# Dilated attention: order of the combination, of the transposes and of the last half-tiles

## The chip, the cores and the metric

The kernel runs on one core of a Trainium2 chip. The metric is the device time of one execution in microseconds (us), the median of several runs. The core has five engines with queues of their own: TensorE (PE in the profile, its weight loads PEld), VectorE (DVE), ScalarE (ACT), GpSimd (POOL) and SyncE (SP), which here issues the DMA transfers. Each engine works through its instructions in the order in which they stand in its queue, and semaphores hold an instruction back until what it needs is there.

## The reference

One encoder block on a sequence of 1024 tokens with 1024 channels. Three mixers work side by side on the normalised input: a dilated window attention, a grouped-query attention with rotary positions, and a cross-attention into 256 memory tokens. Each mixer's output is multiplied by a gate, projected by a branch matrix (`w_br_a`, `w_br_b`, `w_br_m`), merged with sigmoid gates and projected by `w_out`; a norm and the residual follow. All data are float32.

The change concerns the dilated attention. It has three groups of eight heads, with window and dilation (128, 1), (512, 4) and (2048, 16); each gives an output and a log-denominator per token and head, and the three are combined by a softmax over the log-denominators:

```python
for gi, (window, dil) in enumerate(A_GROUPS):
    hs = slice(gi * A_HEADS, (gi + 1) * A_HEADS)
    o_g, lse_g = dilated_window_attention(aq[:, :, hs], ak[:, :, hs], av[:, :, hs], window, dil)
    outs.append(o_g)
    lses.append(lse_g)
wts = jax.nn.softmax(jnp.stack(lses, axis=0), axis=0).astype(dt)
oa = jnp.einsum('gbsh,gbshd->bshd', wts, jnp.stack(outs, axis=0)).reshape(b, s, BRANCH_WIDTH)
...
ya = (oa * jax.nn.silu(ga)) @ w_br_a[layer]
```

## The kernel before

A float32 product runs on TensorE as three products of a high and a low part (high x high, high x low, low x high). The parts come from "splits": ScalarE copies the high part (L1342 for a weight tile, L1863 `dl_high` for a mixer's output), and another engine subtracts it to get the low part (L1343 on VectorE or GpSimd, L1866 `dl_low` on GpSimd).

From L887 on the order of the instructions on every engine is the order in which the program writes them. The stage in question (L1992, `weave(16, every(), ...)`, about 1062 to 1264 us after the span's start) interleaves two streams by counters of cost. One stream is sixteen branch projections (`add_y(m)`, m = 0 to 15, matmuls at L1885, 24 each). Around them run the load of a weight tile, its split (on GpSimd for m + 1, so the split of m = 14 is due during m = 13), the load of a gate and the evacuation on VectorE (L1360 to L1365); these are kept in a list `pend`, of which one is taken after every second matmul.

The other stream is the attention, in twelve items n = 0 to 11: pairs of heads p_ = 0 to 3, for each the groups g = 0 to 2. An item has eight blocks of 128 queries, T = 0 to 7. It runs as a software pipeline over the previous item `pre` and the current one `it`, in four visits b = 0 to 3, each followed by two "rest" pieces T = 2b and 2b + 1. A visit puts on TensorE the scores of two blocks (L1561 to L1573), and transposes of probabilities of an earlier pair of blocks (L1608): of the previous item in visits 0 and 1, of the current one in visits 2 and 3. VectorE masks the scores (L1585) and copies the transposes (L1614); ScalarE takes the exponential (L1586). In visit 1 the previous item's statistics are transposed and copied by ScalarE (`stats`, L1663 to L1670, into the tile sr). In visit 2 the previous item's values are multiplied (`pv`, matmuls L1627 or L1637 to L1647, evacuated by ScalarE at L1657), and the values of the current item are loaded (tile avs). Banks of PSUM come from rings; `pst()` hands out the next of four.

After the third group of a pair of heads is through, its combination begins with visit 2 of the item that follows. Its steps are a list in `combine`, and `STEP_T` gives for each step the piece T at which it is written: fetch the statistics (SyncE), `shares` (VectorE L1798 to L1801, ScalarE), `weights` (VectorE), `put` (SyncE L1814), the loads of two weight tiles wgt (SyncE L1786), `weigh(0)` and `weigh(1)` (products on GpSimd, L1822), `weigh(1, True)` (a sum on GpSimd, L1820), `load(2)`, `load_gate` (L1830), `weigh(2)`, its sum, `gate` (GpSimd L1825) and `store` (SyncE L1833). The tile wgt has two buffers, so a later load waits until an earlier product is done. A step that is written at a T smaller than its predecessor's is that of the next item. The stored parts come back as hl and are split by `dl_high` and `dl_low`.

The last pair of heads (p_ = 3) is combined without memory. TensorE spreads the weights over PSUM banks (`wide(g, x)`, for group g and half x of the columns), `first_two(x)` adds the first two groups, and `third(x)` adds the third on VectorE (L1971, L1972), multiplies by the gate on GpSimd (L1973) and splits the half (L1863, L1866). The list in `ending()` sets their order. Behind the stage, projections m = 16, 17 and 18 start at L2027 with half of their products each, in three pairs of PSUM banks, two of which hold spreads of the last pair of heads.

Of the kernel before, what the change touches and what calls it, by code (L numbers as in the profile page):

```python
# [9 lines left out]
R = mybir.dt.float32r  # L10
# [5 lines left out]
S = 1024  # L16
NT = 8
P = 128
# [15 lines left out]
def block(ctx: ExitStack, tc: tile.TileContext, x, xT, memT, cst, msk, bcst, tabA, gpost,  # L34
          wu, wv, wb, wmem, wbr, wout, out):
    nc = tc.nc
    V, A, G, PE = nc.vector, nc.scalar, nc.gpsimd, nc.tensor
# [10 lines left out]
    bank = {}  # L48
# [14 lines left out]
    def pss1():  # L63
        return bank["p"].tile([P, 512], F32, name="s1", tag="s1", bufs=bank["n"][1])

    def pst():
        bank["i"] += 1
        return bank["p"].tile([P, 4, 128], F32, name="tr", tag="t", bufs=bank["n"][2])
# [149 lines left out]
    def pool(name, side="left"):  # L218
        p = tc.tile_pool(name=name, bufs=1, side=side, reuse_waits="tile")
        return p, p.__enter__()  # L220
# [673 lines left out]
    qkp, qk = pool("qk")  # L894
# [25 lines left out]
    def parts_of(t):  # L920
        return t if type(t) is tuple else (t[:, lo], t[:, hi])
# [289 lines left out]
    for n in range(28):  # L1211
        i, k = divmod(n, 4)
# [47 lines left out]
    for n in range(28):  # L1260
        i, k = divmod(n, 4)
# [77 lines left out]
    def y_split(m, E=V, t=None):  # L1339
        if m < len(steps):  # L1340
            t = t or wp.tile([P, 1024], R, name="wh")
            A.activation(t[:, lo], YW[m][:, lo], AF.Copy)  # L1342
            E.tensor_tensor(t[:, hi], YW[m][:, lo], t[:, lo].bitcast(F32), op=OP.subtract)  # L1343
            YW[m] = [z.rearrange("p (k f) -> p k f", k=4) for z in parts_of(t)]
# [126 lines left out]
    with ExitStack():  # L1471
# [10 lines left out]
        def pickers():  # L1482
            i96 = ident[0:96, 0:96]
            V.tensor_reduce(pick, i96.rearrange("p (x t) -> p t x", t=NT), axis=AX.X, op=OP.add)
            V.tensor_reduce(each, i96.rearrange("p (x t) -> p x t", t=NT), axis=AX.X, op=OP.add)
            V.tensor_tensor(each[:, 0:6], each[:, 0:6], each[:, 6:12], op=OP.add)
            V.tensor_copy(spread.rearrange("p g h q -> p (g h) q"), each[:, 0:6, None].to_broadcast([96, 6, 64]))

        def qk_fetch(p_, g):

            d = OPS[p_, g] = {}
            for j, x in enumerate("qk"):
                d[x] = qk.tile([P, S], F32, name="a" + x, bufs=2)
                nc.sync.dma_start(d[x], qkd[j, p_, g])
# [197 lines left out]
        def plan(it, pre, nxt):  # L1692

            out = []

            def combining(T):
                while todo and T == todo[0][0]:
                    todo.pop(0)[1]()

            def tokens(T):  # L1700
                n = seq.index(it["key"])
                if (n, T) == (1, 7):
                    pickers()
                if 1 <= n <= 4 and 4 <= T <= 6:
                    (lambda: b_high(n - 1, lo), lambda: b_high(n - 1, hi), lambda: b_low(n - 1))[T - 4]()
                if (n, T) in ((0, 2), (0, 6), (1, 3), (2, 3)):
                    b_load(((0, 2), (0, 6), (1, 3), (2, 3)).index((n, T)))
                if n in (8, 9) and T == 5:
                    dl_load(n - 8)
                if n in (9, 10) and T < 3:  # L1710
                    dl_high(n - 9, half[T]) if T < 2 else dl_low(n - 9)
                if n == 11:
                    if T == 6:
                        DL["g"] = cb.tile([P, S], F32, name="wgt", bufs=2)
                        nc.sync.dma_start(DL["g"], g2d[0, 3])
                    if T in (2, 3):
                        j = T - 2
                        nc.sync.dma_start(rows[32 * j:32 * j + 32], std[3, j].rearrange("s h (t a) -> (s h t) a", t=NT))

            def ready():  # L1720
                if pre and pre["key"][1] == 2:
                    todo.extend(zip(STEP_T, combine(pre["key"][0], [OG.pop((pre["key"][0], x)) for x in range(3)])))

            def visit(b):
                at = it if b > 1 else pre

                def turning():
                    return at["trans"]((b + 2) % 4) if at and (it or b < 2) else []

                copies = turning() if b == 1 or not it else []  # L1730
                if it:
                    it["scores"](b)
                if b == 2 and pre:
                    pre["pv"]()
                for f in copies:
                    f()
                copies = turning() if b != 1 and it else []
                if b == 1 and pre and it:
                    pre["stats"]()
                if it:  # L1740
                    it["soft"](2 * b)
                    it["soft"](2 * b + 1)
                for f in copies:
                    f()
                if not it:
                    return
                if b == 2:
                    it["values"]()
                if b == 2 and pre:
                    ready()  # L1750
                if b == 3 and it["ahead"]:
                    qk_fetch(*it["ahead"])

            def rest(T):
                if T == 3 and pre:
                    pre["send"]()
                combining(T)
                if T == 5 and it["key"][1] < 2:
                    it["turned"]()
                tokens(T)  # L1760

            for b in range(4):
                out.append((lambda b=b: visit(b), SOFT + 100.0 if it else 0.5 * LAST_PAD))
                if not it:
                    out.append((lambda b=b: shares_3(b), 0.5 * LAST_PAD))
                else:
                    out += [(lambda T=T: rest(T), 0.5 * SOFT + 50.0) for T in (2 * b, 2 * b + 1)]
            return out
# [67 lines left out]
                    lambda: weigh(1, True), lambda: load(2), load_gate, lambda: weigh(2), lambda: weigh(2, True), gate] + [store] * (p_ < 2)  # L1836

        todo = []
        STEP_T = (5, 0, 2, 3, 3, 7, 0, 1, 1, 4, 5, 6, 7, 1)
        seq = [(p_, g) for p_ in range(4) for g in range(3)]  # L1840
        items = [item(*x) for x in seq] + [None]

# [4 lines left out]
        def b_load(k):  # L1847
            nc.sync.dma_start(OPER[1][1][k].bitcast(F32), od[1, k])

        def b_high(k, t):  # L1850
            h, l = [x[k][:, t] for x in OPER[1]]
            A.activation(h, l.bitcast(F32), AF.Copy)

        def b_low(k):
            h, l = [x[k] for x in OPER[1]]
            G.tensor_tensor(l, l.bitcast(F32), h.bitcast(F32), op=OP.subtract)

        def dl_load(k):
            nc.sync.dma_start(hl[k].bitcast(F32), od[0, k])
            DL[k] = hl[k].bitcast(F32)  # L1860

        def dl_high(k, t=slice(0, S)):
            A.activation(hh[k][:, t], DL[k][:, t], AF.Copy)  # L1863

        def dl_low(k, t=slice(0, S)):
            G.tensor_tensor(hl[k][:, t], DL[k][:, t], hh[k][:, t].bitcast(F32), op=OP.subtract)  # L1866
# [86 lines left out]
                dl_low(2)  # L1953

        def wide(g, x):
            while (g == 2 or x) and bank["i"] % 4 != (2 + x if g == 2 else g):
                pst()
            W3B[g, x] = pst().rearrange("p a b -> p (a b)") if g == 2 or x else pss1()
            PE.matmul(W3B[g, x], spread[:, g].rearrange("p h q -> p (h q)"), C["w"][0:96, half[x]], start=True, stop=True)

        def first_two(x):
            t = half[x]
            a, b = C["ogs"]
            V.tensor_tensor(W3B[0, x], W3B[0, x], a[:, t], op=OP.mult)
            V.tensor_tensor(a[:, t], W3B[1, x], b[:, t], op=OP.mult)
            V.tensor_tensor(a[:, t], W3B[0, x], a[:, t], op=OP.add)

        def third(x):
            t = half[x]
            a, b = C["ogs"][0], OG[3, 2]  # L1970
            V.tensor_tensor(W3B[2, x], W3B[2, x], b[:, t], op=OP.mult)  # L1971
            V.tensor_tensor(a[:, t], W3B[2, x], a[:, t], op=OP.add)  # L1972
            G.tensor_tensor(a[:, t], a[:, t], DL["g"][:, t], op=OP.mult)  # L1973
            dl_high(3, t)
            dl_low(3, t)

        def ending():
            DL[3] = C["ogs"][0]
            return [(lambda: [wide(g, 0) for g in range(2)], 500.0), (lambda: [wide(g, 1) for g in range(2)], 500.0),
                    (lambda: [first_two(0), wide(2, 0)], 2500.0), (lambda: [first_two(1), wide(2, 1)], 2500.0),  # L1980
                    (lambda: [third(0), y_split(18, V, qk.tile([P, S], R, name="aq", bufs=2))], 2500.0),
                    (lambda: third(1), 2500.0)]

        def every():
            yield from first()
# [358 lines left out]
```

## Time and profile before

| | |
|---|---|
| median of three runs | 1389.47 us (1388.53 to 1391.44) |
| profiled execution | 1393.69 us |
| its span | 1391.9 us |
| mean granted TensorE clock | 0.993 |
| TensorE busy | 1361.3 us, 98% of the span |
| VectorE busy | 1013.2 us, 73% |
| ScalarE busy | 653.8 us, 47% |
| GpSimd busy | 579.7 us, 42% |

The profile is of one execution. Times count from the start of its span; 1.8 us of the execution lie around the span. An instruction is named by the line of the kernel that wrote it, by its engine, and by its tiles as "out<-in". A bracket at the end of a row says how long the engine was idle before it and what ended that. A row of waits reads: who waited, for whom, us in total, how often, the longest. A row of windows gives a stretch of time with the busy time of each engine in it and the TensorE clock that was granted, 1.00 being full speed.

### The profile page before, as it was taken

What the parts mean: (1) busy time and instruction counts of PE and PEld (TensorE: products, weight loads), DVE (VectorE), ACT (ScalarE), POOL (GpSimd) and SP (SyncE); (2) the same over time, 40 slices, a digit from 0 to 9 for tenths busy, and PEclk for the clock granted to TensorE, in tenths of its full rate; (3) what the DMA queues carried; (4) which work ended last, traced back from release to release, by engine and by line L of the source; (5) the groups of instructions that cost most, each with busy time, mean ns of one, the idle gap of its engine ahead of it and who ended that gap; (6) DMA issues with size and microseconds to landing.
All of it is one profiled execution on the core that took longest, in us unless ns stands there. A gap on an engine that the chain in (4) does not pass through costs nothing.

```text
span 1391.9 us, 22846 instructions
## 1 busy us (share of the span) xinstructions
PE 1361.3 (98%) x8303; PEld 1091.7 (78%) x8303; DVE 1013.2 (73%) x1840; ACT 653.8 (47%) x1384; POOL 579.7 (42%) x443
## 2 busy tenths in 40 slices
PE   7999999999999999999999999999999999998997
PEld 7799987666666789988888888888887777777886
DVE  7768767777777498766787776688777667667977
ACT  6454456656655345323333334333335776652332
POOL 0507702676576100254556554456551244561003
PEclk9999999999999999999999999999999999999999
DMA  6355532222244678524233333333338777876455
GB/s 233 97 192 188 187 123 102 99 79 93 72 130 140 218 232 262 173 68 135 78 114 117 111 108 119 121 114 100 96 122 268 241 201 226 264 198 207 148 190 182
DMA packets 125489, 213.81 MB, mean 154 GB/s; under 512 B 32480, under 2 KB 64576, under 8 KB 125376
## 3 DMA queue, kind: packets, MB, share of 16 engines
q1 hardware_dynamic: 116064, 198.42, 44.4%
q10 hardware_dynamic: 9312, 13.93, 2.8%
q8 instruction: 65, 1.06, 0.3%
q14 instruction: 48, 0.39, 0.1%
HBM read 145.92 MB, written 66.38 MB: 153 GB/s over the span
## 4 chain that ended last, share of the span: by engine, by line
PE 84%; DMA 4%; DVE 3%; POOL 3%; ACT 2%; issue 2%; SPq 1%; DVEq 0%; POOLq 0%; ACTq 0%
PE s L1309 35%; PE d L1885 4%; PE s L1219 4%; PE s L2109 4%; PE ov L804 3%; PE sc L2027 3%; PE s L1270 3%; PE d L128 3%; PE d L132 3%; PE d L130 3%; PE tr L770 2%; PE s L789 2%; PE s L788 2%; DMA avs<-vdr 2%; PE d L2109 2%
## 5 line engine op out<-in xcount | busy, mean ns | idle before, releaser
L795 POOL TENSOR_TENSOR bl<-bl,bp 128x512 f32<-128x512 f32 x96 | 133.1, 1386 | 54.2 <-ACT bp L791 48.7
L1309 PE MATMUL s<-hh,vS 128*128 128x512 f32 x400 | 133.4, 395 | 0.0
L1309 PE MATMUL s<-vA,vS 128*128 128x512 f32 x450 | 106.6, 390 | 0.0
L91 DVE TENSOR_TENSOR vS<-vot,vS 128x512 fp32r<-128x512 f32 x75 | 86.2, 1150 | 19.9 <-ACT vS L90 19.9
L1309 PEld LDWEIGHTS s<-vA,vS 128*128 128x128 f32 x450 | 84.5, 188 | 18.3
L791 ACT ACTIVATE bp<-s 128x512 f32<-128x512 f32 x128 | 75.7, 596 | 43.6 <-PE s L789 42.5
L771 DVE TENSOR_REDUCE bn<-tr 128x1 f32<-128x512 f32 x128 | 84.9, 683 | 13.4 <-PE tr L770 12.0
L1585 DVE CUSTOM_DVE_ANT_0 pra<-s,mask 128x192 f32<-128x192 f32 (+1 forms) x192 | 49.7, 309 | 59.9 <-PE s L1573 26.3
L128 PE MATMUL d<-hh,wh 128*128 128x512 f32 x224 | 90.0, 402 | 2.4 <-DVE fth L201 2.4
L132 PE MATMUL d<-hh,wl 128*128 128x512 f32 x224 | 90.1, 402 | 0.0
L130 PE MATMUL d<-hl,wh 128*128 128x512 f32 x224 | 89.3, 399 | 0.0
L1309 PEld LDWEIGHTS s<-hh,vS 128*128 128x128 f32 x400 | 75.3, 188 | 17.7
L1586 ACT ACTIVATE pra<-pra,sts 128x192 f32<-128x192 f32 (+1 forms) x176 | 72.4, 414 | 16.0 <-DVE sts L1585 15.8
L1309 PE MATMUL s<-hl,vS 128*128 128x512 f32 x200 | 79.1, 395 | 0.0
L1309 PE MATMUL s<-hh,wh 128*128 128x512 f32 x200 | 78.4, 392 | 0.0
L1309 PE MATMUL s<-hh,wl 128*128 128x512 f32 x200 | 78.4, 392 | 0.0
L1309 PE MATMUL s<-hl,wh 128*128 128x512 f32 x200 | 77.8, 389 | 0.0
L1313 ACT ACTIVATE vv<-s 128x512 f32<-128x512 f32 x50 | 30.0, 599 | 85.6 <-PE s L1309 59.1
L1053 POOL TENSOR_TENSOR vot<-wr 128x512 f32<-128x512 f32 x13 | 22.2, 1705 | 111.8 <-DVE wl L91 111.8
L804 PE MATMUL ov<-bp,VS 128*64 128x512 f32 x256 | 58.5, 598 | 0.0
L1053 POOL TENSOR_TENSOR vot<-vot,vA 128x512 f32<-128x512 f32 x12 | 19.3, 1609 | 90.7 <-DVE vS L91 90.7
L128 PEld LDWEIGHTS d<-hh,wh 128*128 128x128 f32 x224 | 42.6, 190 | 16.3 <-issue 5.5
(627 smaller groups left out, 4016.2 us busy)
## 6 DMA issues: line engine op xcount, KB each, us to landing
wr<-in_wu SPq DMA_DIRECT2D x40, 512.0 KB
vA<-in_wu SPq DMA_DIRECT2D x24, 512.0 KB
qkd<-ko SPq DMA_DIRECT2D x96, 128.0 KB
wl<-thd SPq DMA_DIRECT2D x24, 512.0 KB
wos<-os SPq DMA_DIRECT2D x12, 512.0 KB
wr<-in_wbr SPq DMA_DIRECT2D x24, 256.0 KB
aq<-qkd SPq DMA_DIRECT2D x12, 512.0 KB
ak<-qkd SPq DMA_DIRECT2D x12, 512.0 KB
```

What stands on the lines that cost most here:

```text
L91: V.tensor_tensor(dst_l, src, dst_h.bitcast(F32), op=OP.subtract)
L128: PE.matmul(dst, wh[:, k, :], hh[k][:, t], start=k == 0, stop=False)
L130: PE.matmul(dst, wh[:, k, :], hl[k][:, t], start=False, stop=False)
L132: PE.matmul(dst, wl[:, k, :], hh[k][:, t], start=False, stop=k == 7)
L771: fp["last"] = V.tensor_reduce(st[i]["n"][:, j, c:c + 1], s, axis=AX.X, op=OP.min)
L791: A.activation(pp, s, AF.Exp, scale=-1.0)
L795: G.tensor_tensor(lsum[i % 2], lsum[i % 2], pp, op=OP.add)
L804: PE.matmul(o[e * 64:e * 64 + 64], VS[:, kt, kv], d.pop(kt), start=kt < 2, stop=kt >= NT - 2)
L1219: PE.matmul(now[j], a, b, start=k == 0 and q == 0, stop=k == 3 and q == 2)
L1309: PE.matmul(BANK[n, c], a, b, start=k == 0 and q == 0 and not more, stop=k == 3 and q == 2, skip_group_check=c in "XW")
L1586: A.activation(src, src, AF.Exp, scale=-1.0, bias=bias, accum_out=sts[:, 1, h, T:T + 1])
L2109: PE.matmul(dst[:, e[0]:e[1]], a, b, start=k == 0 and q == 0, stop=k == 3 and q == 2)
```

## The change

Four things are moved; no arithmetic is added or removed.

1. In visit 2 the transposes of the current item's first two blocks are written before the previous item's values; before, they were written after them.
2. `STEP_T` has other pieces. Listed by step: `shares` T 0 to 1, `weigh(0)` 7 to 6, `weigh(1)` 0 of the next item to 7, its sum 1 to 0, `load(2)` 1 to 0, `load_gate` 4 to 3, `weigh(2)` 5 to 3, its sum 6 to 4, `gate` 7 to 6. Fetch, weights, put, the first loads and the store stay where they were.
3. The spreads of the last combination are put at other places of the ring of banks.
4. The two halves of the third term follow each other, and the split of weight tile m = 18 comes after the second half; before, it stood between the halves.

```diff
@@ visit
                 if it:
                     it["scores"](b)
-                if b == 2 and pre:
-                    pre["pv"]()
                 for f in copies:
                     f()
                 copies = turning() if b != 1 and it else []
+                if b == 2 and pre:
+                    pre["pv"]()
@@ combine
-        STEP_T = (5, 0, 2, 3, 3, 7, 0, 1, 1, 4, 5, 6, 7, 1)
+        STEP_T = (5, 1, 2, 3, 3, 6, 7, 0, 0, 3, 3, 4, 6, 1)
@@ wide
-            while (g == 2 or x) and bank["i"] % 4 != (2 + x if g == 2 else g):
+            while (g == 2 or x) and bank["i"] % 4 != {(0, 1): 3, (1, 1): 1, (2, 0): 2, (2, 1): 0}[g, x]:
                 pst()
@@ ending
-                    (lambda: [third(0), y_split(18, V, qk.tile([P, S], R, name="aq", bufs=2))], 2500.0),
-                    (lambda: third(1), 2500.0)]
+                    (lambda: third(0), 2500.0),
+                    (lambda: [third(1), y_split(18, V, qk.tile([P, S], R, name="aq", bufs=2))], 2500.0)]
```

## The prediction

> **What bounds the kernel now.** I read the page's busy times first, then TensorE's grouped waits over the stage that the change touches (us 860 to 1290 hold nothing else that stops TensorE for long), then the windows around these waits, then the timelines of single engines there.
>
> ```profile
> PE 1361.3 (98%) x8303; PEld 1091.7 (78%) x8303; DVE 1013.2 (73%) x1840; ACT 653.8 (47%) x1384; POOL 579.7 (42%) x443
> ```
> ```profile
> PE sc L2027 <- DVE og L1972: 3.6, 1, 3.6
> PE tr L1637 <- DMA avs<-vdr: 2.6, 3, 2.0
> PE s L1565 <- DVE sts L1585: 1.8, 2, 1.1
> PE tr L1608 <- ACT sr L1670: 1.5, 1, 1.5
> PE d L1885 <- POOL wh L1343: 0.3, 1, 0.3
> ```
>
> TensorE is busy 98% of the span, so only what changes a wait of TensorE, or its clock, changes the time. The second view (total us, times, longest us) lists all there is to win directly: 3.6 + 2.6 + 1.8 + 1.5 + 0.3 = 9.8 us. The clock adds to that. In the windows the columns are PE, PEld, DVE, ACT, POOL busy, granted clock, DMA share, GB/s:
>
> ```profile
> 1199.00:1202.41 3.41, 1.88 (x20) 1.50 (x17) 1.17 (x6) 3.02 (x12) 3.41 (x3) 1.00 1.04 413
> 1202.41:1205.82 3.41, 3.41 (x35) 2.42 (x34) 2.26 (x8) 3.41 (x11) 1.83 (x1) 0.50 0.83 281
> 1212.65:1216.06 3.41, 2.34 (x23) 1.78 (x21) 3.22 (x16) 1.85 (x6) 0.62 (x1) 1.00 0.94 324
> 1216.06:1219.47 3.41, 3.41 (x100) 3.10 (x100) 0.63 (x5) 1.54 (x7) 1.74 (x1) 1.00 0.90 309
> 1229.72:1233.13 3.41, 1.27 (x20) 1.03 (x22) 0.38 (x4) 0.00 (x0) 3.33 (x2) 1.00 1.09 310
> 1233.13:1236.54 3.41, 3.41 (x55) 2.85 (x52) 0.22 (x3) 0.49 (x1) 1.44 (x1) 0.50 0.44 92
> 1263.85:1267.26 3.41, 3.19 (x8) 2.55 (x9) 2.13 (x4) 1.95 (x4) 2.52 (x2) 0.50 0.72 228
> ```
>
> After a window with 1.53 us idle (3.41 − 1.88) or 2.14 us idle (3.41 − 1.27), and after the 3.6 us wait, the next 3.41 us are granted 0.50; after one with 1.07 us idle (3.41 − 2.34) they are granted 1.00. So a stall costs its own length, and from somewhere between 1.07 and 1.53 us inside one window also a slow stretch behind it.
>
> What a slow stretch costs, and the other TensorE rows (start, duration, waits in brackets):
>
> ```profile
> 1197.91 1.11 PE L1627 MATMUL tr<-app,avs 64*64 64x64 f32 x64
> 1200.75 0.52 PE L1608 MATMUL tr<-cs,pra 64*128 64x64 f32 x10 [1.53 <-ACT sr L1670]
> 1232.30 2.51 PE L1637 MATMUL tr<-app,avs 128*64 128x128 f32 x28 [1.97 <-DMA avs<-vdr]
> 1235.81 0.48 PE L1608 MATMUL tr<-cs,pra 64*128 64x64 f32 x4
> 1238.33 0.34 PE L1608 MATMUL tr<-cs,pra 64*128 64x64 f32 x4
> 1244.00 0.40 PE L1885 MATMUL d<-bh,wh 128*128 128x512 f32 x1
> 1257.54 0.39 PE L2027 MATMUL sc<-hh,wh 128*128 128x512 f32 x1
> 1260.07 0.39 PE L2027 MATMUL sc<-hh,wh 128*128 128x512 f32 x1
> 1264.07 0.76 PE L2027 MATMUL sc<-hh,ak 128*128 128x512 f32 x1 [3.61 <-DVE og L1972]
> 1268.39 0.39 PE L2027 MATMUL sc<-hh,aq 128*128 128x512 f32 x1
> ```
>
> The same four transposes take 0.48 us at clock 0.50 and 0.34 us at 1.00, so 0.29 of their slow time is lost. Over a stretch that is at least 3.41 × 0.29 = 1.0 and at most 3.41 × 0.50 = 1.7 us. I take 1.3.
>
> **The change, part by part.** Four edits, each costed on the profiled execution (1393.69 us, span 1391.9), which is 4.2 us above the median of the three runs (1389.47); the sum is then taken off the median. No instruction is added or removed on any engine, nor any DMA (allocations that only turn the ring of banks aside), so every term is a wait that moves.
>
> *Gate one piece earlier.* The 0.3 us wait for GpSimd's L1343 (the split of m = 8, which stands behind the gate there) goes: −0.3.
>
> *Transposes ahead of values, third visit.* The ten transposes at 1200.75 take 0.52 us and wait for the statistics' copy, which ScalarE does late, behind dl_high. Today the values' 64 matmuls (1.11 us) are issued before that wait and use the time; afterwards they stand behind it and the transposes. What is in cover becomes exposed: 1.11 − 0.52 = +0.6. The 1.53 us itself and its slow stretch stay. Where the values wait for a load (1232.30), it is the other way: the four transposes (0.34) fill the wait, −0.35. The same happens in front of 1184.60 (0.45 us in a timeline row), but what follows there waits again, so I take 0. The VectorE waits of L1565 (1.8) keep their work ahead: 0, bounded by −1.8 and, if all of the transposes' copies come late instead, +0.6.
>
> *Combination's steps.* SyncE's queue holds the rest: the store of a finished part waits there for the gate, and everything behind it on SyncE (weights out, loads of weights, values) with it.
>
> ```profile
> SPq L1833 <- POOL og L1825: 9.5, 2, 5.0
> ```
>
> The store waits 9.5 us in two places. The gate one piece earlier takes about 1.0 us off that chain, and with it off the landing of the values that TensorE waits for at 1232.30. Bounds: −2.16 (all of 1.97 and of the 0.19 just ahead of it) and +0.6, if the gate's load, which now goes ahead of the values' loads on SyncE, delays them by its own issue. I take −1.0, as the queue ahead is the nearest row. With the 0.35 that leaves 0.8 us idle, under the 1.07 that did no harm, so the slow stretch of 1233.13 goes too: −1.3. Running sum: −0.3 + 0.6 − 0.35 − 1.0 − 1.3 = −2.35.
>
> Then a wait is added. On GpSimd the split of m = 14 stands today between the third product and the last sum; afterwards the sum is ahead of it:
>
> ```profile
> 1237.86 2.96 POOL L1822 TENSOR_TENSOR og<-og,wgt 128x1024 f32<-128x1024 f32 x1 [3.29 <-DMA wgt<-wgd]
> 1240.75 1.30 POOL L1343 TENSOR_TENSOR wh<-wr,wh 128x512 fp32r<-128x512 f32 x1
> 1242.00 2.40 POOL L1820 TENSOR_TENSOR og<-og 128x1024 f32<-128x1024 f32 x1
> ```
>
> The product starts at its load's landing, 1237.86 − 1.0 for the earlier chain = 1236.9; + 2.96 + 2.40 + 1.30 = 1243.5. TensorE needs the split at its third matmul of m = 14, today at 1244.00, then at 1244.0 − 2.35 = 1241.65. That is a new stall of 1.9 us, and the gain up to there shrinks to −0.45. Bounds: no stall if the load lands 1.9 us earlier (−2.35), a stall of 2.9 if it lands no earlier (+0.55). With 1.7 us of the idle time in the window 1239.95 to 1243.36 (the grid of the windows above) a slow stretch follows: +1.3.
>
> *The third term's halves in a row, and the banks.* Today the split of m = 18 (ScalarE copy, VectorE L1343) stands between the halves on VectorE; it waits 2.59 us for ScalarE's copy, that one stands behind dl_high, which waits for GpSimd. The second half, and the bank that m = 17 wants, come only after it.
>
> ```profile
> 1256.62 0.69 DVE L1972 TENSOR_TENSOR og<-tr,og 128x512 f32<-128x512 f32 x1
> 1259.90 1.36 DVE L1343 TENSOR_TENSOR aq<-wr,aq 128x512 fp32r<-128x512 f32 x1 [2.59 <-ACT aq L1342]
> 1261.18 0.68 DVE L1363 SCALAR_TENSOR_TENSOR d<-wl,d 128x512 f32<-128x512 f32 x1
> 1261.90 0.69 DVE L1365 TENSOR_TENSOR acc<-d,acc 128x512 f32<-128x512 f32 x1
> 1263.23 0.69 DVE L1972 TENSOR_TENSOR og<-tr,og 128x512 f32<-128x512 f32 x1
> ```
> ```profile
> 1258.72 0.63 ACT L1863 ACTIVATE hh<-og 128x512 fp32r<-128x512 f32 x1 [5.50 <-POOL og L1973]
> 1259.26 0.61 ACT L1342 ACTIVATE aq<-wr 128x512 fp32r<-128x512 f32 x1
> ```
> ```profile
> 1257.39 1.29 POOL L1973 TENSOR_TENSOR og<-og,wgt 128x512 f32<-128x512 f32 x1 [3.44 <-DVE og L1972]
> 1259.43 1.28 POOL L1866 TENSOR_TENSOR hl<-og,hh 128x512 fp32r<-128x512 f32 x1 [0.74 <-ACT hh L1863]
> ```
>
> Afterwards VectorE ends half 0 at 1257.31, does the two evacuations (1.4), and ends half 1 at 1257.31 + 1.4 + 1.4 = 1260.1. m = 17 would start on TensorE at 1260.3 (m = 16's last matmul, 1260.07, + 0.23), so its 3.61 us wait goes whichever bank it has; the new bank numbers I cost at 0 for that reason, and if half 1 were not done they would cost up to the 3.6. Late next is m = 18's split. GpSimd: half 0 to 1258.7, its dl_low to 1260.7, half 1's product to 1262.05. ScalarE: dl_high to 1262.7, the copy to 1263.2. VectorE's L1343 then runs beside GpSimd's dl_low, as the row above did (1.36), to 1264.65. m = 18 starts at 1264.75. TensorE would be there at 1260.3 + 2.76 = 1263.06 (2.76 is m = 16's 1257.54 to 1260.30), so 1.7 us of stall. Today m = 18 starts at 1268.39: −3.64. Bounds: −4.3 with L1343 at 0.68, and −2.1 if a slow stretch follows the new stall (today's m = 17 took 4.32 instead of 2.76, so 1.5 lost). The stall lies across the edge at 1263.85, 0.8 in one window and 0.9 in the other: I take none.
>
> **Sum**: −0.45 + 1.3 − 3.64 = −2.8. Against the profiled execution 1390.9; against the median 1389.47 − 2.8 = 1386.7.
>
> **The rivals.**
> 1. *Neither stall is followed by a slow stretch*: −0.45 − 3.64 = −4.1, 1385.4. For it: the stalls of 1.9 and 1.7 us fall on windows whose place I can't know in another run. Against it: 1.53 us sufficed in the trace. The Trainium skill ("TensorE: Matmul & The Clock Gate", section "Why this matters for your kernels") asks for no idle gaps over about 3 us between bursts; by that rule stalls of 1.9 us would bring no slow stretch and this rival holds. The trace does not agree: 0.50 was granted after 1.53 us of idle.
> 2. *Both are followed by one*: −4.1 + 1.3 + 1.5 = −1.3, 1388.2. For it: both stalls exceed 1.53 if each lies in one window.
> 3. *The split of m = 14 is in time*, because the earlier loads move by 1.9 us more: −2.35 − 3.64 = −6.0, 1383.5. Against it: SyncE's transfers share nearly all of the DMA (share 1.09 in the window from 1229.72), so issue earlier is not landing earlier.
> 4. *The tail is not freed* (the change does not do what it says): m = 17 finds its bank taken as before, since the split now needs the same engines later. −0.45 + 1.3 = +0.85, 1390.3. Against it: half 1 ends 0.2 us before m = 17 is due; for it: only 0.2 us.
> 5. *Slower*: values behind transposes in every item. If at the other ten visits too the transposes wait for a bank that the statistics or the shares hold, each pays the 0.6 of 1200.75: ten × 0.6 = 6.0, so −2.8 + 6.0 = +3.2, 1392.7. It decides from five such visits on (3.0 > 2.8). For it: VectorE and ScalarE lag TensorE in these visits (L1565 waits). Against it: of L1608's waits for the statistics' copy only one is in the view.
>
> **How the numbers follow.** Chances: forecast 0.30, rival 1 0.19, rival 2 0.12, rival 3 0.10, rival 4 0.07, rival 5 0.22. The measurement of this kernel can tell about 0.2%, 2.8 us, from no change. The forecast sits on that bound, so half of it counts as faster and half as the same. Faster: 0.15 + 0.19 + 0.10 = 0.44; same: 0.15 + 0.12 + 0.07 = 0.34; slower 0.22. The range runs from 1383.9 to 1392.0: it leaves out most of rival 3 and half of rival 5, together under 0.2. The likeliest case's own range, by its bounds, is 1385.4 to 1388.2.
>
> **What would show it.** m = 17's wait for L1972 is gone from TensorE's waits and m = 18 waits for L1343 instead, about 1.7 us; two L1971/L1972 pairs stand ahead of VectorE's aq. TensorE's wait for avs at 1232 is under 1.1 us and the following window at clock 1.00. On GpSimd L1820 stands ahead of the split of m = 14, and TensorE waits for L1343 there for about 2 us. The statistics' wait at 1200 is as long as before, with the values behind it. The prediction is wrong if waits of VectorE or ScalarE grow in visits that are quiet today, if the values' loads land later than now, or if a slow stretch stands where none is forecast.

## The result

The changed kernel takes 1386.77 us (median of 8 runs, 1384.58 to 1387.79), the kernel before in the same series 1390.69 us (8 runs, 1388.53 to 1393.73). The ratio is 0.9971 with a 95% interval of 0.9960 to 0.9982: faster by 4.0 us (2.5 to 5.6). The profiled execution of the changed kernel takes 1387.79 us, its span 1386.0 us, mean granted clock 0.998.

TensorE's grouped waits after, over the same stretch as the prediction's (us 860 to 1290; total us, times, longest us):

```profile
PE d L1885 <- POOL wh L1343: 2.3, 2, 1.5
PE s L1565 <- DVE sts L1585: 1.7, 2, 1.2
PE tr L1627 <- ACT sr L1670: 1.4, 1, 1.4
PE tr L1637 <- DMA avs<-vdr: 1.2, 2, 0.7
PE s L1923 <- DVE acc L1365: 0.7, 1, 0.7
PE sc L2027 <- DVE aq L1343: 0.7, 1, 0.7
```

The 3.6 us wait of m = 17 for L1972 is gone, and 0.7 us for L1343 at m = 18 stands in its place. The wait for the values (L1637) is down from 2.6 to 1.2 us; on SyncE the store's waits for the gate are down from 9.5 to 7.4 us:

```profile
SPq L1833 <- POOL og L1825: 7.4, 2, 4.0
```

The wait for GpSimd's splits (L1885 for L1343) is up from 0.3 to 2.3 us, a wait of 0.7 us at L1923 is new, and the statistics' copy is now waited for inside the values' matmuls (L1627) instead of the transposes.

TensorE's timeline after, at the places that the prediction costed (start, duration, wait in brackets):

```profile
1158.73 0.50 PE L1885 MATMUL d<-bh,wh 128*128 128x512 f32 x1 [0.83 <-POOL wh L1343]
...
1228.92 0.44 PE L1637 MATMUL tr<-app,avs 128*64 128x128 f32 x4 [0.71 <-DMA avs<-vdr]
1229.81 0.44 PE L1637 MATMUL tr<-app,avs 128*64 128x128 f32 x4 [0.44 <-DMA avs<-vdr]
...
1242.14 0.50 PE L1885 MATMUL d<-bh,wh 128*128 128x512 f32 x1 [1.50 <-POOL wh L1343]
...
1255.75 0.39 PE L2027 MATMUL sc<-hh,wh 128*128 128x512 f32 x1
...
1261.41 0.50 PE L2027 MATMUL sc<-hh,aq 128*128 128x512 f32 x1
1261.76 0.39 PE L2027 MATMUL sc<-hl,aq 128*128 128x512 f32 x1
1262.81 0.73 PE L2027 MATMUL sc<-hh,aq 128*128 128x512 f32 x2 [0.66 <-DVE aq L1343]
```

The tail, from the first matmul of m = 16 to the third of m = 18, takes 1262.81 − 1255.75 = 7.06 us. Before it took 1268.39 − 1257.54 = 10.85 us to the first of m = 18, and two more matmuls of 0.23, 11.3 us. So the tail gave 4.2 us between the two profiles. Ahead of it, the stage is 0.95 us shorter (the tail begins 1257.54 − 1255.75 = 1.79 us earlier, and 0.84 us of that were there when the stage began, at 1061.57 instead of 1062.41).

GpSimd and VectorE after, at m = 14 and m = 18:

```profile
1238.48 2.38 POOL L1820 TENSOR_TENSOR og<-og 128x1024 f32<-128x1024 f32 x1
1240.82 1.26 POOL L1343 TENSOR_TENSOR wh<-wr,wh 128x512 fp32r<-128x512 f32 x1
```
```profile
1261.39 1.36 DVE L1343 TENSOR_TENSOR aq<-wr,aq 128x512 fp32r<-128x512 f32 x1 [3.21 <-DMA wB<-wod]
```

The sum stands ahead of the split of m = 14, as forecast. VectorE's split of m = 18 comes after both halves.

The window in which the new stall at m = 14 lies, and the next one (columns as in the prediction):

```profile
1239.54:1242.95 3.41, 1.91 (x30) 1.13 (x32) 2.56 (x9) 0.21 (x1) 3.41 (x3) 1.00 1.06 307
1242.95:1246.36 3.41, 3.41 (x67) 2.85 (x57) 1.48 (x3) 2.54 (x4) 1.47 (x1) 1.00 0.86 332
```

No slow stretch follows the 1.50 us of idle time. In the whole stage the changed kernel's profile has none, where that of the kernel before has three. The two profiled executions differ by more (1393.69 − 1387.79 = 5.9 us) than the medians: that of the kernel before lies 3.0 us above its median, that of the changed kernel 1.0.

### The profile page after: what moved, and what is told of

It reads as the page before. It is cut to its first block, busy times and chain, and to the rows that moved or that the text cites. A ratio compares the mean times of both kernels' runs of the same rounds, so it can differ in the third digit from the quotient of the medians.

```text
span 1386.0 us, 22874 instructions
## 1 busy us (share of the span) xinstructions
PE 1357.5 (98%) x8303; PEld 1088.2 (79%) x8303; DVE 1013.2 (73%) x1840; ACT 654.0 (47%) x1384; POOL 579.3 (42%) x443
## 4 chain that ended last, share of the span: by engine, by line
PE 85%; DMA 3%; DVE 3%; POOL 3%; ACT 2%; issue 2%; SPq 1%; DVEq 0%; POOLq 0%; ACTq 0%
PE s L1309 35%; PE d L1885 4%; PE s L1219 4%; PE s L2109 4%; PE ov L804 3%; PE s L1270 3%; PE sc L2027 3%; PE d L128 3%; PE d L130 3%; PE d L132 3%; PE tr L770 2%; PE s L789 2%; PE s L788 2%; PE d L2109 2%; POOL bl L795 1%
```

## The experiments

All runs were compared with runs of the kernel before on the same chip. "Faster by" is worked out from the ratio and 1390.5 us.

### Each edit alone

The third term's halves in a row, nothing else:

```diff
-                    (lambda: [third(0), y_split(18, V, qk.tile([P, S], R, name="aq", bufs=2))], 2500.0),
-                    (lambda: third(1), 2500.0)]
+                    (lambda: third(0), 2500.0),
+                    (lambda: [third(1), y_split(18, V, qk.tile([P, S], R, name="aq", bufs=2))], 2500.0)]
```

> Only the fourth edit on the kernel before: third term's halves in a row, split of m = 18 after them. Theory (the gain is mostly this edit): TensorE's wait of 3.6 us for L1972 at m = 17 is gone, a wait of 0.7 to 1.7 us for L1343 at m = 18 stands in its place, no slow stretch behind it; 3.6 to 4.5 us faster than before. Rival (the new bank numbers are needed for it): m = 17 still waits over 3 us for L1972, within 1 us of before.

1386.98 us, ratio 0.9973 (0.9964 to 0.9983): faster by 3.8 us. TensorE's waits in this run:

```profile
PE tr L1637 <- DMA avs<-vdr: 1.7, 1, 1.7
PE s L1565 <- DVE sts L1585: 1.6, 2, 1.1
PE s L1959 <- DVE wgt L1947: 1.3, 1, 1.3
PE tr L1608 <- ACT sr L1670: 1.3, 1, 1.3
PE sc L2027 <- DVE aq L1343: 0.7, 1, 0.7
```

m = 17 waits no longer, although the spreads lie in the old banks. This edit alone is the whole gain of the change, within the intervals.

This run also shows how far single waits go without any edit. Up to the tail it has the instructions of the kernel before in the same order, and so has the next run, with the bank numbers alone. Still the waits for the values are 2.6 us before, 1.7 here and 2.4 there; for the statistics' copy 1.5, 1.3 and 0.7; at L1959 0.2, 1.3 and 0.6. Ahead of the tail the kernel before has two slow stretches, this run has none, and the next run has a single one. So one wait in one profile, or one slow stretch, says little about an edit where the differences are of this size.

The bank numbers alone:

```diff
-            while (g == 2 or x) and bank["i"] % 4 != (2 + x if g == 2 else g):
+            while (g == 2 or x) and bank["i"] % 4 != {(0, 1): 3, (1, 1): 1, (2, 0): 2, (2, 1): 0}[g, x]:
```

> Only the third edit on the kernel before: the spreads' bank numbers. Theory (the bank numbers do nothing by themselves): m = 17 still waits about 3.6 us for L1972, within 0.5 us of before. Rival (the banks free m = 17): that wait is under 0.5 us and the kernel 3 to 5 us faster.

1390.36 us, ratio 0.9998 (0.9989 to 1.0008). The wait stands as it was:

```profile
PE sc L2027 <- DVE og L1972: 3.6, 1, 3.6
```

So the bank numbers do nothing by themselves, and the halves don't need them.

The steps alone:

```diff
-        STEP_T = (5, 0, 2, 3, 3, 7, 0, 1, 1, 4, 5, 6, 7, 1)
+        STEP_T = (5, 1, 2, 3, 3, 6, 7, 0, 0, 3, 3, 4, 6, 1)
```

> Only the second edit on the kernel before: STEP_T. Theory (gain at the values' wait, paid back at GpSimd's queue): TensorE's wait for the values at 1232 shrinks from 2.0 us to about 1.0 and the slow stretch behind it goes (together about 2.3 us), but m = 14 waits 1.5 to 2 us for the split behind the sum on GpSimd, and m = 8 about 0.5 us more than before; within 1.5 us of before. Rival (the steps carry the gain): over 2.5 us faster.

1391.24 us, ratio 1.0001 (0.9992 to 1.0011). TensorE's waits:

```profile
PE sc L2027 <- DVE og L1972: 3.6, 1, 3.6
PE d L1885 <- POOL wh L1343: 3.1, 3, 1.4
PE s L1565 <- DVE sts L1585: 1.7, 2, 1.2
PE s L1923 <- DVE acc L1365: 1.1, 1, 1.1
PE tr L1608 <- ACT sr L1670: 1.1, 1, 1.1
```

The wait for the values has left the list (2.6 us before), and 3.1 us for GpSimd's splits and 1.1 us at L1923 have come: in this profile the gain is paid back, as expected.

The order in the third visit alone:

```diff
-                if b == 2 and pre:
-                    pre["pv"]()
                 for f in copies:
                     f()
                 copies = turning() if b != 1 and it else []
+                if b == 2 and pre:
+                    pre["pv"]()
```

> Only the first edit on the kernel before: transposes ahead of values in visit 2. Theory (it costs where the statistics' copy is late and pays where the values' load is late): values instead of transposes wait at 1200, +0.3 to +0.6 us; at 1232 the wait is about 0.35 us shorter; within 1 us of before. Rival (it moves VectorE's and ScalarE's work so that other visits wait): 2 us or more slower.

1391.94 us, ratio 1.0003 (0.9994 to 1.0013): between 0.8 us faster and 1.8 us slower, so a large loss is excluded; by the medians it is 1.5 us slower. TensorE waits 2.7 us for the statistics' copy in the values, and 1.8 us of its 2.3 us for the values stand in one piece. Against the kernel before that is 1.2 us more for the statistics' copy, where 0.3 to 0.6 was expected, and 0.3 less for the values:

```profile
PE tr L1627 <- ACT sr L1670: 2.7, 1, 2.7
PE tr L1637 <- DMA avs<-vdr: 2.3, 2, 1.8
```

The four ratios alone add up to −3.8 − 0.3 + 0.1 + 0.4 = −3.6 us; the whole change measures −4.0.

### Two edits taken out of the whole

Without the steps (`STEP_T` as before, the other three edits):

> The changed kernel without the second edit: STEP_T as before, the other three edits. Theory (the new steps win at the values' wait near 1230 and lose it at m = 8 and m = 14): no wait for L1343 at m = 14, a wait of 1.5 us or more for the values near 1230 and one of 0.5 to 1.3 us for L1947 at L1959; within 1 us of the changed kernel. Rival (the steps are worth their gain once the tail is freed): 2 us or more slower than the changed kernel.

1387.94 us, ratio 0.9975 (0.9965 to 0.9985), by the ratios 0.6 us slower than the changed kernel, which the intervals don't tell from none. The forecast of L1959 came (1.2 us for L1947). That of the values did not: their wait was 0.7 us here, so in this combination the steps weren't needed to shorten it. As expected, no wait for L1343 is left in the list.

Without the order (values ahead of transposes, the other three edits):

> The changed kernel without the first edit: values ahead of transposes as before, the other three edits. Theory (the first edit costs): 0.5 to 2 us faster than the changed kernel. Rival (the late gates and stores carried the gain of old_order_gates_late): within 0.5 us of the changed kernel.

1387.30 us, ratio 0.9975 (0.9966 to 0.9985): no faster than the changed kernel. The theory that the first edit costs found no support in this combination; TensorE's listed waits add up to 7.4 us against 8.3 in the changed kernel, a difference that the times don't show.

### GpSimd's queue

The last sum and the gate of p_ = 2 one piece later, so that the split of m = 14 is ahead of the sum:

```diff
-                    todo.extend(zip(STEP_T, combine(
+                    todo.extend(zip(STEP_T[pre["key"][0]], combine(
...
-        STEP_T = (5, 1, 2, 3, 3, 6, 7, 0, 0, 3, 3, 4, 6, 1)
+        STEP_T = ((5, 1, 2, 3, 3, 6, 7, 0, 0, 3, 3, 4, 6, 1), (5, 1, 2, 3, 3, 6, 7, 0, 0, 3, 3, 4, 6, 1),
+                  (5, 1, 2, 3, 3, 6, 7, 0, 0, 3, 3, 6, 7))
```

> The changed kernel with the steps of the last whole pair of heads (p_ = 2) one piece apart again: the sum at T 6 and the gate at T 7, so that GpSimd does the split of m = 14 ahead of the sum. Theory (TensorE's 1.5 us wait for the split hides another wait: the last spreads' weights tile waits for the gate on GpSimd, which ends no earlier): the wait for L1343 at m = 14 goes, a wait of about 1.2 us for L1947 at L1959 takes its place, 0.3 us faster than the changed kernel. Rival (the 1.5 us are simply won): no wait at L1959, 1.5 us faster than the changed kernel.

1386.07 us, ratio 0.9970 (0.9957 to 0.9983), level with the changed kernel by the ratios. The wait at m = 14 is gone and a wait of only 0.20 us stands at L1959, less than the theory's 1.2, so the rival's first half was right in the profile; the medians differ by 0.7 us, within the intervals. GpSimd's timeline in this run:

```profile
1236.85 1.29 POOL L1343 TENSOR_TENSOR wh<-wr,wh 128x512 fp32r<-128x512 f32 x1
1238.09 2.38 POOL L1820 TENSOR_TENSOR og<-og 128x1024 f32<-128x1024 f32 x1
```

The split of m = 14 on VectorE:

```diff
-                    pend.append(lambda: y_split(m + 1, G))
+                    pend.append(lambda: y_split(m + 1, V if m == 13 else G))
```

> The changed kernel with the split of m = 14 on VectorE instead of GpSimd, steps as changed. GpSimd then does product, sum and gate in a row and ends the gate about 1.3 us earlier. Theory (GpSimd's queue from the third product to the gate sets TensorE's end of this part): no wait at m = 14, a wait under 0.5 us at L1959, 1.0 to 1.5 us faster than the changed kernel. Rival (VectorE is held up by the split's wait for ScalarE): the scores' waits of L1561 or L1565 near 1235 grow by 0.5 us or more and nothing is won.

1387.38 us, ratio 0.9981 (0.9971 to 0.9992), no gain. The rival's mechanism came at another place: TensorE waits 1.7 us at L1923. VectorE's split waits for ScalarE's copy, then takes 2.32 us, and the masking behind it is late:

```profile
1234.62 2.32 DVE L1343 TENSOR_TENSOR wh<-wr,wh 128x512 fp32r<-128x512 f32 x1 [3.04 <-ACT wh L1342]
```

The split computed twice, which only lengthens the stall:

```diff
+            if m == 14:
+                E.tensor_tensor(t[:, 512:1024], YW[m][:, 0:512], t[:, 0:512].bitcast(F32), op=OP.subtract)
             E.tensor_tensor(t[:, hi], YW[m][:, lo], t[:, lo].bitcast(F32), op=OP.subtract)
```

> The changed kernel with the split of m = 14 computed twice on GpSimd (1.28 us more in its queue). Theory (a stall brings a slow stretch only when at least 1.53 us of it falls into one window of 3.41 us): the wait at m = 14 is about 2.8 us, the next window is granted 0.50, and the kernel is 1.3 + 1.0 to 1.7 = 2.3 to 3.0 us slower than the changed kernel. Rival (stalls under 3 us bring no slow stretch): 1.3 us slower, clock 1.00 all through the stage.

1389.85 us, ratio 0.9987 (0.9977 to 0.9996): 1389.85 − 1386.77 = 3.1 us slower than the changed kernel by the medians, 2.2 us by the ratios, whose intervals still overlap a little. The stall was 2.34 us, and the two windows behind it were granted half the clock:

```profile
1237.24:1240.65 3.41, 1.62 (x9) 0.98 (x9) 2.74 (x10) 0.41 (x2) 3.33 (x3) 1.00 1.04 295
1240.65:1244.06 3.41, 2.87 (x66) 2.31 (x67) 0.09 (x1) 0.06 (x1) 2.81 (x2) 0.50 0.83 296
1244.06:1247.47 3.41, 3.41 (x9) 2.60 (x10) 1.28 (x2) 3.35 (x5) 0.51 (x1) 0.50 0.18 70
```

This is the nearest to a test of the clock alone: the same kernel with 0.84 us more of a stall (2.34 − 1.50) loses 2.2 to 3.1 us and shows a slow stretch, twice as long as expected, that the changed kernel's profile does not have. Less the 0.84 us, that leaves 1.4 to 2.3 us for two slow windows. The mean clock of all runs agrees: 0.996 over the ten here, 0.998 over the changed kernel's eight. The rival, that a stall under 3 us brings no slow stretch, fell.

### A faster version

Gate and store of p_ = 0 and 1 put behind the splits on GpSimd, the last sum and gate as above; first edit left out:

```diff
-        STEP_T = (5, 1, 2, 3, 3, 6, 7, 0, 0, 3, 3, 4, 6, 1)
+        STEP_T = ((5, 1, 2, 3, 3, 6, 7, 0, 0, 3, 3, 4, 2, 4), (5, 1, 2, 3, 3, 6, 7, 0, 0, 3, 3, 4, 2, 4),
+                  (5, 1, 2, 3, 3, 6, 7, 0, 0, 3, 3, 6, 7))
```

> Third and fourth edit, no first edit (values ahead of transposes as before), new steps with gate and store of p_ = 0 and 1 put behind the splits on GpSimd (gate at T 2, store at T 4 of the item after) and those of p_ = 2 at T 6 and T 7. Theory (first edit costs 0.3 us, splits behind gates 0.8 us at m = 8): no wait for L1343 at m = 8, 11 and 14, 0.5 to 1.5 us faster than the changed kernel. Rival (the first edit is what fills the values' wait at 1229): a wait for the values of 1.5 us or more near 1229, no faster than the changed kernel.

1383.10 us (5 runs, 1382.51 to 1384.85), ratio 0.9947 (0.9933 to 0.9960): faster than the kernel before by 7.4 us and, by the medians, than the changed one by 3.7 (by the ratios 3.3). This version beats both kernels. TensorE's waits:

```profile
PE s L1565 <- DVE sts L1585: 1.7, 2, 1.2
PE s L1923 <- DVE acc L1365: 1.2, 1, 1.2
PE sc L2027 <- DVE aq L1343: 0.7, 1, 0.7
PE tr L1627 <- DMA avs<-vdr: 0.3, 1, 0.3
```

No split, no statistics' copy and no load of L1637's values is waited for any more. The rival (a wait of 1.5 us for the values) did not come. On SyncE the store no longer stands in front of the next sends and loads while it waits for the gate. In the changed kernel it did, from about 1196 to 1200.04, with the values' and statistics' transfers behind it; here they go first. SyncE's timelines, the changed kernel and this one:

```profile
1195.57 0.39 SPq L1350 DMA_DIRECT2D wl<-thd  x1
1200.04 0.32 SPq L1833 DMA_DIRECT2D od<-og  x1
1200.45 0.66 SPq L1685 DMA_DIRECT2D std<-sr  x1
```
```profile
1193.08 0.48 SPq L1350 DMA_DIRECT2D wl<-thd  x1
1196.35 0.33 SPq L1685 DMA_DIRECT2D std<-sr  x1
1196.79 0.37 SPq L1518 DMA_DIRECT2D avs<-vdr  x1
1198.63 0.33 SPq L1833 DMA_DIRECT2D od<-og  x1
```

The same with the first edit:

> All four edits, with the steps of the run old_order_gates_late (gate and store of p_ = 0 and 1 at T 2 and T 4 of the item after, last sum and gate at T 6 and T 7); so the first edit, transposes ahead of values, is the only difference from that run. Theory (the first edit costs): a wait of 0.5 us or more stands again within the values' matmuls near 1197, for the statistics' copy, and the kernel is 0.5 to 2 us slower than old_order_gates_late. Rival (the late gates and stores carry the 3.7 us that run won over the changed kernel): within 0.5 us of old_order_gates_late, 1383 us.

1384.64 us, ratio 0.9959 (0.9944 to 0.9975). Its profile has a wait of 1.1 us for the statistics' copy again, at L1627, as the theory had it; of the 1.5 us between the medians the intervals, which overlap, make no certainty. By the medians the late gates and stores give 2.1 us of the 3.7 (1386.77 − 1384.64), but the intervals of this run and the changed kernel overlap too. Clear of noise is the pair without the first edit: without_order, 1387.30 us (ratio from 0.9966), and old_order_gates_late, 1383.10 us (up to 0.9960), differ only in the steps. Of these, the part for p_ = 2 alone won nothing measurable (split_before_sum), so the gates and stores of p_ = 0 and 1 carry most of it. Whether leaving the first edit out pays with them isn't shown.

ScalarE's copy for m = 18 put between the third term's halves, on top of the faster version:

```diff
+        def high_18():
+            C["t"] = qk.tile([P, S], R, name="aq", bufs=2)
+            A.activation(C["t"][:, lo], YW[18][:, lo], AF.Copy)
+
+        def low_18():
+            t = C["t"]
+            V.tensor_tensor(t[:, hi], YW[18][:, lo], t[:, lo].bitcast(F32), op=OP.subtract)
+            YW[18] = [z.rearrange("p (k f) -> p k f", k=4) for z in parts_of(t)]
...
-                    (lambda: third(0), 2500.0),
-                    (lambda: [third(1), y_split(18, V, qk.tile([P, S], R, name="aq", bufs=2))], 2500.0)]
+                    (lambda: [third(0), high_18()], 2500.0),
+                    (lambda: [third(1), low_18()], 2500.0)]
```

> The run old_order_gates_late with ScalarE's copy for the split of m = 18 put between the third term's halves, VectorE's subtraction still after both. The subtraction then follows the second half at once. Theory: TensorE's 0.66 us wait for L1343 at m = 18 goes, 0.7 to 1.0 us faster than old_order_gates_late. Rival (VectorE's aq slows the second half's GpSimd product, or another wait takes its place): within 0.3 us.

1383.03 us, ratio 0.9949 (0.9935 to 0.9963): the same as the version without it. The wait at m = 18 is gone from TensorE's list, but the profile has 0.7 us for the statistics' copy instead (the 1.3 us at L1923 were 1.2 in the version without it), and whether the 0.7 us was won can't be told from these runs. VectorE's subtraction, now at L1983, takes as long as before. GpSimd's product of the second half, which it overlaps, is longer than its 1.29 us, as the rival had it:

```profile
1254.82 1.38 DVE L1983 TENSOR_TENSOR aq<-wr,aq 128x512 fp32r<-128x512 f32 x1
```
```profile
1255.60 1.75 POOL L1973 TENSOR_TENSOR og<-og,wgt 128x512 f32<-128x512 f32 x1
```

## Why the prediction was right, point by point

The forecast was 1386.7 us and the measured median 1386.77; against the kernel before, −2.8 was forecast and −4.0 (2.5 to 5.6) measured. The direction is right and the interval contains the forecast size. The path was right at the tail, which is where the change won. Ahead of the tail it was not the likeliest case that came but rival 1 (no slow stretch, −4.1, chance 0.19). That the two absolute numbers agree to 0.1 us is luck: the longer series puts the kernel before at 1390.69, not 1389.47, and single terms were off by up to 1.3 us one way and 0.9 us the other.

- **The third term's halves** (−3.64): right in mechanism, and shown by the run with this edit alone. Mis-sized by 0.6: 4.2 us measured. The step that failed is "m = 18 starts at 1264.75". Only the third matmul of m = 18 needs the subtracted part; the first two ran at 1261.41 and 1261.76, and the stall was 0.66 us instead of 1.7. The chain of engines up to the split was right: put 1.79 us later, for the earlier start of the tail, VectorE's L1343 ends at 1264.5 (forecast 1264.65), and it took 1.36 us as forecast.
- **The bank numbers** (0): right; alone they change nothing, and the halves work without them.
- **The values' wait** (−0.35, −1.0 and its slow stretch −1.3): the size is about right, the cause open. From 2.16 us at two places (0.19 and 1.97) it fell to 1.15 (0.71 and 0.44; 0.8 was forecast), and no slow stretch came. The store's longest wait on SyncE went from 5.0 to 4.0 us, the 1.0 that was forecast. But the run without the new steps has a shorter wait still (0.7), and the run with the halves alone has no slow stretch there either, though nothing ahead of the tail was moved in it. So −1.3 is a property of one execution and not of the edit.
- **Transposes ahead of values** (+0.6): the place was right. The values' matmuls now wait 1.4 us for the statistics' copy. That its slow stretch would stay was wrong in this profile; those 1.39 us were split over two windows. In the run with the order alone the wait grew by 1.2 us, twice the forecast.
- **The split of m = 14** (+1.9, then a slow stretch of +1.3): the stall came with 1.50 us, TensorE's row naming L1343 of GpSimd. The slow stretch did not: 1.91 us of the window were busy. This and the slow stretch behind the statistics' wait are the steps that failed by most, 1.3 us each. With 0.84 us more of a stall the stretch came (split_twice).
- **The gate one piece earlier** (−0.3 at m = 8): wrong. The wait grew from 0.27 to 0.83 us. The gate was written earlier, but GpSimd's third product started at its load's landing, 1149.28 before and 1149.58 after, and sum, gate and split follow it in a row. Moved up in a queue that waits for a load, the gate came no earlier. Seen from TensorE, whose stage began 0.84 us earlier in this execution (1061.57 instead of 1062.41), it came later. The faster version, which puts the split ahead of the gate, is what removed the wait.
- **Not forecast**: 0.67 us at L1923 for L1365. This and the wait at m = 8 are no larger than what single waits differ by without an edit (see the halves alone).
- **The rivals.** Rival 4 (tail not freed) and rival 5 (values behind transposes in every item) fell: the tail gave 4.2 us, and the order alone costs between −0.8 and +1.8 us. Rival 3 (the split in time) fell, the stall was there. Between the forecast and rival 1 (no slow stretch, −4.1) the measured −4.0 and the changed kernel's profile speak for rival 1, but not for the Trainium skill's rule that stood beside it ("TensorE: Matmul & The Clock Gate", section "Why this matters for your kernels"), since single stalls of 1.5 us (before), 1.7 us (the split on VectorE), 2.2 us (the bank numbers alone) and 2.3 us (the split twice) did bring slow stretches.

On the profiled executions, for which the terms were worked out, the sum did not hold: −2.8 was forecast for the stage, and −0.95 − 4.2 = −5.2 came. Terms that were too favourable (m = 8, off by 0.9; L1923, 0.7) were outweighed by those that were too harsh (two slow stretches that did not come, 1.3 each; the tail, 0.6; the stall of m = 14, 0.4). A sum that met the profiles would have missed the median, since that execution of the kernel before was a long one, with three slow stretches in the stage. The run with the halves alone says more plainly what carried the change: 3.8 of 4.0 us.

## What to carry to other kernels

When one engine is busy 98% of the span, list its waits and ask of each what is queued ahead of the releaser on the releaser's engine: the largest gain here was VectorE's wait for a copy, with work queued behind it that did not need the copy. Moving steps earlier in a queue won nothing that could be measured here; what won was moving late-needed steps (gates, stores) behind early-needed ones (splits, loads). And cost a stall together with the clock: here a stall that fell on two windows cost no clock, and a shorter one inside one window did.

## What was not expected of the hardware

By these profiles, whether TensorE gets half the clock depends on how busy it was in one window of 3.41 us, on a fixed grid, and not on the length of a single gap. In the profile of the kernel before, the three slow stretches begin at 1202.41, 1233.13 and 1263.85, each 30.72 us after the last, nine times 3.41. Over the profiles of all kernels here, of the windows of this stage that had the full clock those ahead of a slow stretch had at most 1.88 us busy, and those with 1.91 us or more were never followed by one. Nine windows stand ahead of a slow stretch, and in a band from 1.75 to 1.88 us both happen. Windows ahead, and the one behind, of the bank numbers alone, the split on VectorE, the order alone and the run without steps, in this order:

```profile
1222.52:1225.93 3.41, 1.54 (x21) 0.90 (x20) 1.48 (x11) 1.44 (x8) 3.41 (x2) 1.00 1.16 252
1225.93:1229.34 3.41, 2.90 (x26) 2.51 (x28) 0.00 (x0) 0.00 (x0) 3.33 (x2) 0.50 1.09 310
```
```profile
1235.75:1239.16 3.41, 1.75 (x10) 1.19 (x10) 3.41 (x15) 1.44 (x8) 3.33 (x2) 1.00 0.75 160
1239.16:1242.57 3.41, 3.41 (x46) 2.42 (x49) 2.93 (x13) 0.41 (x2) 2.38 (x2) 0.50 1.02 357
```
```profile
1198.61:1202.02 3.41, 1.86 (x63) 1.69 (x64) 1.21 (x3) 3.22 (x12) 3.41 (x2) 1.00 1.01 400
1202.02:1205.43 3.41, 3.41 (x40) 2.64 (x39) 2.31 (x11) 3.41 (x11) 1.21 (x1) 1.00 0.92 293
```
```profile
1195.82:1199.23 3.41, 1.78 (x75) 1.52 (x75) 1.62 (x10) 2.43 (x8) 3.41 (x3) 1.00 1.02 407
1199.23:1202.64 3.41, 3.41 (x43) 2.65 (x40) 2.31 (x7) 3.41 (x11) 2.20 (x1) 1.00 0.87 305
```

With 1.54 and 1.75 us busy the clock fell, with 1.86 and 1.78 us it did not. Where the grid lies differs between executions, so the same 2.7 us wait of the order alone fell on two windows and cost no clock. That this also makes the spread of the kernel before (1388.3 to 1395.6 us in 35 runs) is likely: of those runs the eight with a mean clock of 0.994 took 1391.6 us on average, the seven with 0.997 1389.9. It is not shown, for each kernel has one profile.

VectorE's subtraction of 128x512 took 0.68 us by itself (0.68 to 0.69 us are also the rows of L1363 and L1972 in the prediction), 1.36 us beside GpSimd's subtraction of the same size, and 2.32 us beside GpSimd's product of 128x1024; GpSimd's 128x512 product took 1.75 instead of 1.29 us beside it. Each time VectorE's subtraction ended 0.54 to 0.56 us after GpSimd's instruction (1262.75 and 1262.21 in the changed kernel, 1236.94 and 1236.38 with the split on VectorE, 1256.20 and 1255.65 with the copy early), as if it had waited for it; no run tests that. Not every operation of VectorE is longer: L1365, with one input in PSUM, took 0.69 us from 1256.16, within GpSimd's product from 1255.60 to 1256.89. A subtraction moved to VectorE to relieve GpSimd can therefore cost more than its row alone says.
